# Interleaving the weight slabs so that TensorE loads weights with a step of two, four or eight elements

## The chip, the cores and the metric

The kernel runs on one core of one Trainium2 chip. The metric is the device time of one execution in microseconds (us); lower is better. All matrix work is done on TensorE (PE in the profile, with its weight loads on a row of their own, PEld). VectorE (DVE) and ScalarE (ACT) prepare operands and finish results, SyncE (SP) issues the transfers from device memory.

## What is computed

One layer of a sequence model for 256 time steps of 2048 channels, all in float32. Cut to what matters:

```python
z = rmsnorm(x, g1) @ w_in + b_in              # 2048 -> 7 * 2048
xa, ya, cb, cc, cx, ga, gb = split(z)
xa = rg_lru(causal_conv4(xa))                 # gates: 8 blocks of 256x256
out_a = (xa * gelu(ya)) @ w_pa                # 2048 -> 2048
out_b = (cb * causal_conv3(cc * cx)) @ w_pb   # 2048 -> 2048
x = x + (sigmoid(ga) * out_a + sigmoid(gb) * out_b) @ w_o
u = square(relu(rmsnorm(x, g2) @ w_mlp1))     # 2048 -> 8192
x = x + u @ w_mlp2                            # 8192 -> 2048
return rmsnorm(x, gf)
```

## The kernel before

**Layout.** Channels lie on the 128 partitions and the 256 time steps along the free dimension, so an activation of 2048 channels is 16 tiles of 128 x 256. A weight matrix is cut, on the host, into slabs: a slab holds 8 blocks of 128 x 128 (8 row blocks of one column block), that is 128 partitions x 1024 float32 numbers or 512 KB. In a slab of before, block k takes the columns from k x 128 to k x 128 + 127, one block after the other.

**Two parts for precision.** Every float32 number is split into a high part, rounded to the format that TensorE takes at full speed, and a low part, the remainder. For weights the class `Weights` does this: SP transfers a slab into a `raw` tile (one of 4), ACT casts it into `whi` (L52), DVE subtracts to give `wlo` (L53). There are four buffers of each, and slabs are made three ahead of their use. Activations are held as tiles `a` of 128 x 2 x 256 with the high part in `a[:, 0]` and the low part in `a[:, 1]`.

**The inner loop.** `product` makes one tile of 128 output channels. For each block it runs two matmuls: the *hi* matmul, with the block of `whi` as stationary operand and both parts of the activation as 512 moving columns (L260), and the *lo* matmul, with the block of `wlo` and the high part of the activation, 256 moving columns (L261). Each of the two has a weight load of its own, of 128 x 128 numbers. The result lies in one PSUM bank of 2 x 256 numbers; the lo matmul adds to one of its halves, and `added` (L266, L268) sums the halves. A *pair* below is one hi and one lo matmul.

**Stages**, in this order, with the tiles of 128 outputs and the pairs of each: the first four tiles of w_in, written out in `first_four` (L289, L290) while the slabs are still arriving; the rest of w_in for the branches, with small gate matmuls for the recurrence (L370 to L372) after each group; a merge stage that for each of 16 tiles takes two tiles of w_in, one of w_pb and one of w_pa; w_o; and then w_1 and w_2, each in two halves `h` (32 tiles of w_1, 16 tiles of w_2, twice). A tile from 2048 channels has 16 pairs; a tile of w_2 in one half has 32. The very last tile of w_2 is made in pieces by `rows` (L460, L461), its last 18 blocks for one half of the time steps and then for the other, so that the final norm and the stores of the first half overlap.

**Two irregular places.** In the first half of w_2 every second tile is made `turned`: apart from its first and last block the lo matmul is issued ahead of the hi matmul (L257, L258). And in w_1 the lo matmul adds to half 1 of the bank for h = 0 and to half 0 for h = 1 (`side`).

**The end.** After the last stores are issued, 20 further matmuls run whose result nobody reads (L532, L534). They take blocks of `whi` as stationary operand, and four at a time differ in the weight columns (128 or 32) and in the moving operand (activation, weights, one element broadcast to 512 columns, and bfloat16 ones).

Instructions on each engine run in the order in which the engine was given them; DVE and ACT get their slab splits with a priority that moves them ahead in that order.

Of the kernel before, what the change touches and what calls it, by code (L numbers as in the profile page):

```python
# [9 lines left out]
F32 = mybir.dt.float32  # L10
# [4 lines left out]
P = 128  # L15
S = 256
D = 2048
NT = D // P
# [3 lines left out]
HALF = 8  # L22
# [2 lines left out]
AHEAD = 300  # L25
WAKE = 9
SPLIT = 18

PARAMS = [("g1", NT), ("g2", NT), ("gf", NT), ("b_in", 7 * NT), ("ca_w", 4 * NT), ("ca_b", NT),
          ("br", NT), ("bi", NT), ("lam", NT), ("cb_w", 3 * NT), ("eye", P)]  # L30
# [50 lines left out]
def trunk(ctx: ExitStack, tc: tile.TileContext, xT, xt, par, w_in, w_lru, w_pa, w_pb, w_o, w_1, w_2, out):  # L81
    nc = tc.nc
# [5 lines left out]
    wk = ctx.enter_context(tc.tile_pool(name="wk", bufs=3))  # L88
    psz = ctx.enter_context(tc.tile_pool(name="psz", bufs=6, space=bass.MemoryType.PSUM))
    psl = ctx.enter_context(tc.tile_pool(name="psl", bufs=2, space=bass.MemoryType.PSUM))  # L90
# [6 lines left out]
    def moving(i):  # L97
        return big.tile([P, NT, 2, S], F32R, name="big%d" % i)
# [32 lines left out]
    def pc(name, j):  # L131
        return pr[:, OFF[name] + j:OFF[name] + j + 1]

    def split(dst, src):

        nc.scalar.copy(dst[:, 0, :], src)
        nc.vector.tensor_tensor(dst[:, 1, :], src, dst[:, 0, :].bitcast(F32), ALU.subtract)  # L137

    def scaled_split(dst, src, g):
        nc.scalar.activation(dst[:, 0, :], src, AF.Copy, scale=g)  # L140
        nc.vector.scalar_tensor_tensor(dst[:, 1, :], src, g, dst[:, 0, :].bitcast(F32), ALU.mult, ALU.subtract)
# [12 lines left out]
    def total(parts):  # L154

        ps = psl.tile([P, 512], F32, name="psl")
        for i, sq in enumerate(parts):
            nc.tensor.matmul(ps[:, :S], ones, sq, start=i == 0, stop=i == len(parts) - 1)
        return ps[:, :S]
# [13 lines left out]
    xg = moving(0)  # L173
# [17 lines left out]
    for i in range(NT // 2):  # L191
        load_x(2 * i, 2)
        c, o = divmod(i, HALF // 2)
# [13 lines left out]
    for i, n in enumerate(("xc", "gy", "cb", "cc", "gate0", "gate1", "q", "v")):  # L207
        h, q = divmod(i, 4)
# [5 lines left out]
    def squares(src, j):  # L214

        if j == 0:
            nc.scalar.activation(ssq, src, AF.Square)
        else:
            sq = wk.tile([P, S], F32, name="s")
            nc.scalar.activation(sq, src, AF.Square)  # L220
            nc.vector.tensor_tensor(ssq, ssq, sq, ALU.add)
# [21 lines left out]
        nc.vector.scalar_tensor_tensor(s2, sd, 2.0, s2, ALU.mult, ALU.add)  # L243
        nc.vector.tensor_scalar(s4, s2, -4.0, None, ALU.mult)

    def product(acts, k0, nh, side=1, turned=False):

        ps = psz.tile([P, 2, S], F32, name="psz")
        n = nh * HALF
        for c in range(nh):  # L250
            hi, lo = W.take()
            for k in range(HALF):
                a = acts(k0 + c * HALF + k)
                i = c * HALF + k
                b = slice(k * P, (k + 1) * P)
                if turned and 0 < i < n - 1:
                    nc.tensor.matmul(ps[:, side, :], lo[:, b], a[:, 0, :], start=False, stop=False)  # L257
                    nc.tensor.matmul(ps, hi[:, b], a, start=False, stop=False)  # L258
                else:
                    nc.tensor.matmul(ps, hi[:, b], a, start=i == 0, stop=False)  # L260
                    nc.tensor.matmul(ps[:, side, :], lo[:, b], a[:, 0, :], start=False, stop=i == n - 1)  # L261
        return ps

    def added(ps):
        low = wk.tile([P, S], F32, name="low")
        nc.scalar.copy(low, ps[:, 1, :])  # L266
        t = wk.tile([P, S], F32, name="t")
        nc.vector.tensor_tensor(t, ps[:, 0, :], low, ALU.add)  # L268
        return t
# [4 lines left out]
        nc.scalar.activation(dst, t, func, bias=pc("b_in", j))  # L274

    def z_product():
        return product(lambda k: xg[:, k], 0, 2)

    def z_tile(j, dst, func):
        z_done(z_product(), j, dst, func)  # L280

    def first_four():

        four = [psz.tile([P, 2, S], F32, name="psz") for _ in range(4)]
        for k in range(NT):
            c = slice(k % 2 * P, (k % 2 + 1) * P)
            for m in range(4):
                hi, lo = fhi[:, k // 2, m, c], flo[:, k // 2, m, c]
                nc.tensor.matmul(four[m], hi, xg[:, k], start=k == 0, stop=False)  # L289
                nc.tensor.matmul(four[m][:, 1, :], lo, xg[:, k, 0, :], start=False, stop=k == NT - 1)  # L290
        return four

    early = first_four()

    def first_norm():
# [16 lines left out]
    ua = moving(1)  # L312
    ub = moving(2)
    with places:
# [5 lines left out]
        for g in range(NB):  # L320
# [3 lines left out]
            for m in range(2):  # L324
                j = 2 * g + m
# [5 lines left out]
                c = xc[:, m, :]  # L331
# [17 lines left out]
            for m in range(2):  # L349
                j = 2 * g + m  # L350
# [3 lines left out]
                c = cc[:, m, :]  # L354
# [8 lines left out]
            hi, lo = W.take()  # L363
            gates = []
            for q in range(2):
                ps = psl.tile([P, 2, S], F32, name="psl")
# [6 lines left out]
                t = w1.tile([P, 2, S], F32, name="gate%d" % q)  # L373
# [3 lines left out]
            r, i = gates  # L377
# [21 lines left out]
    mg = big2.tile([P, NT, 2, S], F32R, name="mg")  # L399
    for j in range(NT):  # L400
        sa = wk.tile([P, S], F32, name="s")
        sb = wk.tile([P, S], F32, name="s")
        z_tile(Z_GA + j, sa, AF.Sigmoid)
        z_tile(Z_GB + j, sb, AF.Sigmoid)
        tb = added(product(lambda k: ub[:, k], 0, 2))
        nc.vector.tensor_tensor(sb, sb, tb, ALU.mult)
        ta = added(product(lambda k: ua[:, k], 0, 2))
        nc.vector.tensor_tensor(sa, sa, ta, ALU.mult)
        nc.vector.tensor_tensor(sa, sa, sb, ALU.add)
        split(mg[:, j], sa)  # L410

    xh = moving(0)
    for j in range(NT):
        t = added(product(lambda k: mg[:, k], 0, 2))
        nc.vector.tensor_tensor(x[:, j, :], x[:, j, :], t, ALU.add)
        scaled_split(xh[:, j], x[:, j, :], pc("g2", j))
        squares(x[:, j, :], j)

    for h in range(2):
        u = [big2.tile([P, NT, 2, S], F32R, name="mg") if h == 1 and c == 0 else moving(c + 1) for c in range(2)]  # L420
        for f in range(NF // 2):
            t = added(product(lambda k: xh[:, k], 0, 2, side=1 - h))
            v = wk.tile([P, S], F32, name="s")
            nc.vector.scalar_tensor_tensor(v, t, 0.0, t, ALU.max, ALU.mult)  # L424
            if h == 1:
                nc.vector.tensor_tensor(v, v, rs, ALU.mult)
            split(u[f // NT][:, f % NT], v)
            if h == 0 and f == 0:
                nc.vector.tensor_scalar(rs, total([ssq]), 1.0 / D, EPS, ALU.mult, ALU.add)
                nc.vector.reciprocal(rs, rs)  # L430
        for j in range(NT - h):
            t = added(product(lambda k: u[k // NT][:, k % NT], 0, 4, turned=h == 0 and j % 2 == 1))
            if h == 0:
                nc.vector.tensor_tensor(t, t, rs, ALU.mult)
            nc.vector.tensor_tensor(x[:, j, :], x[:, j, :], t, ALU.add)
            if h == 1:
                squares(x[:, j, :], j)
                if j == NT - 2:
                    nc.scalar.activation(sink, ssq[:, 0:1], AF.Sqrt)
                nc.scalar.activation(x[:, j, :], x[:, j, :], AF.Copy, scale=pc("gf", j))  # L440

    bf4 = wk.tile([P, 512], mybir.dt.bfloat16, name="s")
    bf = bf4[:, :P]
    nc.gpsimd.memset(bf4, 1.0)

    w = [W.take() for _ in range(4)]
    nk = 4 * HALF

    def rows(k0, k1, c, between=()):

        ps = psz.tile([P, 2, S], F32, name="psz")
        for k in range(k0, k1):
            if k in between:
                between[k]()
            hi, lo = w[k // HALF]
            a = u[k // NT][:, k % NT, :, c]
            b = slice(k % HALF * P, (k % HALF + 1) * P)
            nc.tensor.matmul(ps[:, :, c], hi[:, b], a, start=k == k0, stop=False)  # L460
            nc.tensor.matmul(ps[:, 1, c], lo[:, b], a[:, 0, :], start=False, stop=k == k1 - 1)  # L461
        return ps
# [43 lines left out]

    k0 = nk - SPLIT
    got = []
    t = added(rows(0, k0, slice(0, S)))
# [13 lines left out]
    store(1, by, 2, (5, 5, 4), (nc.sync, nc.scalar))  # L523


    hi = w[3][0]
    still = psl.tile([P, 512], F32, name="psl")
    for cols, moved in ((128, u[1][:, 3]), (32, u[1][:, 3]), (128, hi[:, 0:512].rearrange("p (a b) -> p a b", a=2)),
                        (128, u[1][:, 3, 0:1, 0:1].broadcast_to([P, 2, S])), (0, None)):
        for i in range(4):  # L530
            if cols:
                nc.tensor.matmul(still[:cols, :], hi[:, i * P:i * P + cols], moved, start=True, stop=True)  # L532
            else:
                nc.tensor.matmul(still, bf, bf[:, 0:1].broadcast_to([P, 512]) if i > 1 else bf4, start=True, stop=True)  # L534


def _slabs(w):


    k, n = w.shape  # L540
    w = w.reshape(k // (HALF * P), HALF, P, n // P, P)
    return np.ascontiguousarray(w.transpose(3, 0, 2, 1, 4)).reshape(n // P, k // (HALF * P), P, HALF * P)


def _cols(v):
# [33 lines left out]
```

## Time and profile before

| | |
|---|---|
| time, median of 2 runs | 1657.09 us (1656.47 to 1657.7) |
| profiled execution | 1657.53 us, of which its span, first to last instruction, is 1655.4 us |
| PE / PEld busy | 1648.0 us (100%) / 1448.9 us (88%) |
| DVE / ACT busy | 1123.7 us (68%) / 867.1 us (52%) |
| mean granted TensorE clock | 0.998 |
| read from device memory | 310.62 MB, 189 GB/s over the span |

Busy time is the union of an engine's instruction times. Matmuls overlap each other in the trace, since one begins while the one ahead is still draining, so the mean duration of a matmul (392 ns for hi) is longer than the distance from its start to the next start. The distances are what adds up to the span.

### The profile page before, as it was taken

Reading aid. Unit: us, or ns where it says so; the run is one execution under the profiler, and the core shown is the slowest. Engines: PE = TensorE matmul, PEld = TensorE weight load, DVE = VectorE, ACT = ScalarE, POOL = GpSimd, SP = SyncE. Lnnn points to the kernel's source line nnn. Section 1 sums busy time; section 2 is a strip of 40 time slices with the busy share of each in tenths; the row PEclk is TensorE's granted clock in tenths of the full one; section 3 lists DMA queues with packets and bytes.
Section 4 is the critical chain, followed back from the end, with each engine's and each line's share of the span. In section 5 each row is a group of like instructions: output and inputs, shape, how many; then the busy total and the mean of one; then the engine's idle time right before and its main releaser. Section 6 shows DMA issues by size and latency. Waiting matters only on the chain.

```text
span 1655.4 us, 24421 instructions
## 1 busy us (share of the span) xinstructions
PE 1648.0 (100%) x9500; PEld 1448.9 (88%) x9500; DVE 1123.7 (68%) x1628; ACT 867.1 (52%) x1272; POOL 3.9 (0%) x38
## 2 busy tenths in 40 slices
PE   9999999999999999999999999999999999999998
PEld 8888888888888888888888888888888888888887
DVE  5979878978976666566667766665555677765554
ACT  7756666666765444444455444443334444444442
POOL 0000000000000000000000000000000000000000
PEclk9999999999999999999999999999999999999999
DMA  9665555556556555555555555555555555665553
GB/s 310 195 200 190 186 190 189 187 178 204 190 180 192 190 191 187 187 189 189 191 184 191 185 191 190 187 189 188 189 191 190 189 186 189 190 190 191 190 187 95
DMA packets 94228, 314.31 MB, mean 190 GB/s; under 512 B 10016, under 2 KB 18336, under 8 KB 94112
## 3 DMA queue, kind: packets, MB, share of 16 engines
q1 hardware_dynamic: 93184, 312.29, 58.2%
q8 instruction: 74, 1.21, 0.3%
q10 hardware_dynamic: 928, 0.46, 0.1%
q14 instruction: 42, 0.34, 0.1%
HBM read 310.62 MB, written 2.10 MB: 189 GB/s over the span
## 4 chain that ended last, share of the span: by engine, by line
PE 99%; DVE 1%; DMA 0%; issue 0%; SPq 0%; DVEq 0%; ACT 0%
PE psz L260 59%; PE psz L261 30%; PE psz L258 3%; PE psz L257 2%; PE psz L289 1%; PE psz L460 1%; PE psz L290 0%; PE psl L371 0%; PE psl L372 0%; PE psl L370 0%; PE psl L532 0%; DMA raw<-w_in_s 0%; PE psz L461 0%; DVE wlo L53 0%; DVE x L502 0%; DVE v L392 0%
## 5 line engine op out<-in xcount | busy, mean ns | idle before, releaser
L260 PE MATMUL psz<-big,whi 128*128 128x512 f32 x3776 | 1318.7, 392 | 0.2 <-DVE big L137 0.2
L261 PE MATMUL psz<-big,wlo 128*128 128x256 f32 x3776 | 1059.1, 280 | 0.0
L53 DVE TENSOR_TENSOR wlo<-raw,whi 128x1024 fp32r<-128x1024 f32 x576 | 703.2, 1223 | 488.1 <-ACT whi L52 487.4
L52 ACT CAST whi<-raw 128x1024 fp32r<-128x1024 f32 x576 | 604.1, 1049 | 751.2 <-issue 418.1
L260 PEld LDWEIGHTS psz<-big,whi 128*128 128x128 f32 x3776 | 708.9, 188 | 159.7 <-DVE big L137 0.5
L261 PEld LDWEIGHTS psz<-big,wlo 128*128 128x128 f32 x3776 | 709.9, 188 | 0.4
L260 PE MATMUL psz<-mg,whi 128*128 128x512 f32 x496 | 173.5, 393 | 0.0
L261 PE MATMUL psz<-mg,wlo 128*128 128x256 f32 x496 | 138.8, 280 | 0.0
L260 PEld LDWEIGHTS psz<-mg,whi 128*128 128x128 f32 x496 | 93.1, 188 | 21.0 <-DVE mg L137 0.2
L268 DVE TENSOR_TENSOR t<-psz,low 128x256 f32<-128x256 f32 x256 | 105.9, 417 | 2.8 <-ACT low L266 2.8
L261 PEld LDWEIGHTS psz<-mg,wlo 128*128 128x128 f32 x496 | 93.5, 189 | 0.1
L266 ACT COPY low<-psz 128x256 f32<-128x256 f32 x256 | 93.3, 366 | 0.0
L258 PE MATMUL psz<-big,whi 128*128 128x512 f32 x240 | 84.4, 394 | 0.0
L257 PE MATMUL psz<-big,wlo 128*128 128x256 f32 x240 | 67.2, 280 | 0.0
L258 PEld LDWEIGHTS psz<-big,whi 128*128 128x128 f32 x240 | 45.1, 188 | 10.2
L273 DVE TENSOR_TENSOR t<-t,rs 128x256 f32<-128x256 f32 x112 | 47.1, 422 | 2.2
L257 PEld LDWEIGHTS psz<-big,wlo 128*128 128x128 f32 x240 | 45.2, 188 | 0.3
L424 DVE SCALAR_TENSOR_TENSOR s<-t 128x256 f32<-128x256 f32 x64 | 27.2, 425 | 2.1
L382 DVE RECIPROCAL q<-q 128x512 f32<-128x512 f32 x8 | 26.8, 3344 | 0.0
L289 PE MATMUL psz<-big,big 128*128 128x512 f32 x64 | 23.0, 416 | 1.8 <-ACT big L52 1.8
L334 DVE SCALAR_TENSOR_TENSOR xc<-xa,pr,xc 128x256 f32<-128x256 f32 x48 | 22.3, 477 | 0.0
L137 DVE TENSOR_TENSOR big<-s,big 128x256 fp32r<-128x256 f32 x48 | 20.1, 418 | 0.0
(148 smaller groups left out, 662.1 us busy)
## 6 DMA issues: line engine op xcount, KB each, us to landing
raw<-w_s SPq DMA_DIRECT2D x256, 512.0 KB, 4.2
raw<-w_in_s SPq DMA_DIRECT2D x216, 512.0 KB, 3.5
raw<-w_pb_s SPq DMA_DIRECT2D x32, 512.0 KB, 3.6
raw<-w_pa_s SPq DMA_DIRECT2D x32, 512.0 KB, 3.5
raw<-w_o_s SPq DMA_DIRECT2D x32, 512.0 KB, 3.5
raw<-w_in_s SPq DMA_DIRECT2D x16, 256.0 KB, 5.8
raw<-w_lru_s SPq DMA_DIRECT2D x8, 512.0 KB, 3.6
x<-xT SPq DMA_DIRECT2D x8, 256.0 KB, 5.8
```

What stands on the lines that cost most here:

```text
L52: self.nc.scalar.copy(hi, raw)
L53: self.nc.vector.tensor_tensor(lo, raw, hi.bitcast(F32), ALU.subtract)
L257: nc.tensor.matmul(ps[:, side, :], lo[:, b], a[:, 0, :], start=False, stop=False)
L258: nc.tensor.matmul(ps, hi[:, b], a, start=False, stop=False)
L260: nc.tensor.matmul(ps, hi[:, b], a, start=i == 0, stop=False)
L261: nc.tensor.matmul(ps[:, side, :], lo[:, b], a[:, 0, :], start=False, stop=i == n - 1)
L266: nc.scalar.copy(low, ps[:, 1, :])
L268: nc.vector.tensor_tensor(t, ps[:, 0, :], low, ALU.add)
L273: nc.vector.tensor_tensor(t, t, rs, ALU.mult)
L289: nc.tensor.matmul(four[m], hi, xg[:, k], start=k == 0, stop=False)
L382: nc.vector.reciprocal(q, q)
L424: nc.vector.scalar_tensor_tensor(v, t, 0.0, t, ALU.max, ALU.mult)
```

## The change

Each matrix gets a step: 2 for w_in and w_2, 4 for w_pb and w_1, 8 for w_pa and w_o. On the host, the slab's blocks are interleaved in groups of `step`: column 0 of the group's first block, column 0 of the second and so on, then column 1 of each. A block's 128 columns then lie `step` elements apart, and every weight load reads them so. Size, number and order of the slabs, their transfers and their splits stay as they are, and the recurrence's gate weights stay contiguous. `turned` and `side` are gone: the hi matmul always comes first and the lo matmul always adds to half 1. The 20 matmuls at the end and the tile of ones for them are removed.

```diff
+STEP = {"w_in": 2, "w_pa": 8, "w_pb": 4, "w_o": 8, "w_1": 4, "w_2": 2}
...
-    def product(acts, k0, nh, side=1, turned=False):
+    def columns(k, step):
+
+        b = k // step * step * P + k % step
+        return slice(b, b + (P - 1) * step + 1, step)
+
+    def product(acts, k0, nh, step):
...
-                b = slice(k * P, (k + 1) * P)
-                if turned and 0 < i < n - 1:
-                    nc.tensor.matmul(ps[:, side, :], lo[:, b], a[:, 0, :], start=False, stop=False)
-                    nc.tensor.matmul(ps, hi[:, b], a, start=False, stop=False)
-                else:
-                    nc.tensor.matmul(ps, hi[:, b], a, start=i == 0, stop=False)
-                    nc.tensor.matmul(ps[:, side, :], lo[:, b], a[:, 0, :], start=False, stop=i == n - 1)
+                b = columns(k, step)
+                nc.tensor.matmul(ps, hi[:, b], a, start=i == 0, stop=False)
+                nc.tensor.matmul(ps[:, 1, :], lo[:, b], a[:, 0, :], start=False, stop=i == n - 1)
...
-            c = slice(k % 2 * P, (k % 2 + 1) * P)
+            c = columns(k % 2, STEP["w_in"])
...
-            t = added(product(lambda k: xh[:, k], 0, 2, side=1 - h))
+            t = added(product(lambda k: xh[:, k], 0, 2, STEP["w_1"]))
...
-            t = added(product(lambda k: u[k // NT][:, k % NT], 0, 4, turned=h == 0 and j % 2 == 1))
+            t = added(product(lambda k: u[k // NT][:, k % NT], 0, 4, STEP["w_2"]))
...
-            b = slice(k % HALF * P, (k % HALF + 1) * P)
+            b = columns(k % HALF, STEP["w_2"])
...
-    hi = w[3][0]
-    still = psl.tile([P, 512], F32, name="psl")
-    for cols, moved in ((128, u[1][:, 3]), (32, u[1][:, 3]), (128, hi[:, 0:512].rearrange("p (a b) -> p a b", a=2)),
-                        (128, u[1][:, 3, 0:1, 0:1].broadcast_to([P, 2, S])), (0, None)):
...
-def _slabs(w):
+def _slabs(w, step):
...
-    w = w.reshape(k // (HALF * P), HALF, P, n // P, P)
-    return np.ascontiguousarray(w.transpose(3, 0, 2, 1, 4)).reshape(n // P, k // (HALF * P), P, HALF * P)
+    w = w.reshape(k // (HALF * P), HALF // step, step, P, n // P, P)
+    return np.ascontiguousarray(w.transpose(4, 0, 3, 1, 5, 2)).reshape(n // P, k // (HALF * P), P, HALF * P)
```

The order of instructions on DVE, ACT and SP is the same before and after, line numbers aside; POOL loses one fill of a tile with ones. PE's order changes at two places. The first is each second tile of w_2 in the half h = 0. There PE had (output, activation, weights, size; the numbers belong to buffers):

```order
L260 MATMUL psz<-big_9275,whi_11001 128x512
L261 MATMUL psz<-big_9275,wlo_11002 128x256
L257 MATMUL psz<-big_9275,wlo_11002 128x256
L258 MATMUL psz<-big_9275,whi_11001 128x512
L257 MATMUL psz<-big_9275,wlo_11002 128x256
```

and now has, at the same place, with the two lines of `product` renumbered:

```order
L262 MATMUL psz<-big_9275,whi_11001 128x512
L263 MATMUL psz<-big_9275,wlo_11002 128x256
L262 MATMUL psz<-big_9275,whi_11001 128x512
L263 MATMUL psz<-big_9275,wlo_11002 128x256
L262 MATMUL psz<-big_9275,whi_11001 128x512
```

The second block's lo matmul has moved behind its hi matmul, and so on through the tile, so that hi and lo alternate everywhere. The second place is the end of the program. Before, behind the last lo matmul of the last tile, the last sum of squares and the spread of its result:

```order
L461 MATMUL psz<-big_12498,wlo_15700 128x128
L484 MATMUL psl<-ones,s 128x1
L496 MATMUL psl<-pr,cm_15845 128x128
L532 MATMUL psl<-big_12498,whi_15699 128x512 x4
L532 MATMUL psl<-big_12498,whi_15699 32x512 x4
L532 MATMUL psl<-whi_15699 128x512 x4
L534 MATMUL psl<-s 128x512
L574 UNCONDITIONAL_BRANCH
```

and now:

```order
L459 MATMUL psz<-big_12498,wlo_15698 128x128
L482 MATMUL psl<-ones,s 128x1
L494 MATMUL psl<-pr,cm_15843 128x128
L561 UNCONDITIONAL_BRANCH
```

PE now reaches the end of its program right after the spread. The rows do not show the step of a weight load; it stands only in the slices of the diff.

More of the change, by code (lines that the diff above doesn't have):

```diff
@@ L276, in z_product @@
     def z_product():
-        return product(lambda k: xg[:, k], 0, 2)
+        return product(lambda k: xg[:, k], 0, 2, STEP["w_in"])
     def z_tile(j, dst, func):
@@ L404, in trunk @@
         z_tile(Z_GB + j, sb, AF.Sigmoid)
-        tb = added(product(lambda k: ub[:, k], 0, 2))
+        tb = added(product(lambda k: ub[:, k], 0, 2, STEP["w_pb"]))
         nc.vector.tensor_tensor(sb, sb, tb, ALU.mult)
-        ta = added(product(lambda k: ua[:, k], 0, 2))
+        ta = added(product(lambda k: ua[:, k], 0, 2, STEP["w_pa"]))
         nc.vector.tensor_tensor(sa, sa, ta, ALU.mult)
@@ L413, in trunk @@
     for j in range(NT):
-        t = added(product(lambda k: mg[:, k], 0, 2))
+        t = added(product(lambda k: mg[:, k], 0, 2, STEP["w_o"]))
         nc.vector.tensor_tensor(x[:, j, :], x[:, j, :], t, ALU.add)
@@ L440, in trunk @@
                 nc.scalar.activation(x[:, j, :], x[:, j, :], AF.Copy, scale=pc("gf", j))
-    bf4 = wk.tile([P, 512], mybir.dt.bfloat16, name="s")
-    bf = bf4[:, :P]
-    nc.gpsimd.memset(bf4, 1.0)
     w = [W.take() for _ in range(4)]
@@ L523, in trunk @@
     store(1, by, 2, (5, 5, 4), (nc.sync, nc.scalar))
-    hi = w[3][0]
-    still = psl.tile([P, 512], F32, name="psl")
-    for cols, moved in ((128, u[1][:, 3]), (32, u[1][:, 3]), (128, hi[:, 0:512].rearrange("p (a b) -> p a b", a=2)),
-                        (128, u[1][:, 3, 0:1, 0:1].broadcast_to([P, 2, S])), (0, None)):
[L530 to L534, printed above, removed]
-def _slabs(w):
+def _slabs(w, step):
     k, n = w.shape
-    w = w.reshape(k // (HALF * P), HALF, P, n // P, P)
-    return np.ascontiguousarray(w.transpose(3, 0, 2, 1, 4)).reshape(n // P, k // (HALF * P), P, HALF * P)
+    w = w.reshape(k // (HALF * P), HALF // step, step, P, n // P, P)
+    return np.ascontiguousarray(w.transpose(4, 0, 3, 1, 5, 2)).reshape(n // P, k // (HALF * P), P, HALF * P)
 def _cols(v):
@@ L562 @@
             norm1_g, norm2_g, final_g, b_in, conv_a_w, conv_a_b, lru_br, lru_bi, lru_lam, conv_b_w, np.eye(P, dtype=np.float32))], 1)),
-        "w_in_s": _slabs(np.asarray(w_in)[0]),
+        "w_in_s": _slabs(np.asarray(w_in)[0], STEP["w_in"]),
         "w_lru_s": np.ascontiguousarray(lru).reshape(NB, P, HALF * P),
-        "w_pa_s": _slabs(np.asarray(w_pa)[0]),
-        "w_pb_s": _slabs(np.asarray(w_pb)[0]),
-        "w_o_s": _slabs(np.asarray(w_o)[0]),
-        "w_1_s": _slabs(np.asarray(w_mlp1)[0]),
-        "w_2_s": _slabs(np.asarray(w_mlp2)[0]),
+        "w_pa_s": _slabs(np.asarray(w_pa)[0], STEP["w_pa"]),
+        "w_pb_s": _slabs(np.asarray(w_pb)[0], STEP["w_pb"]),
+        "w_o_s": _slabs(np.asarray(w_o)[0], STEP["w_o"]),
+        "w_1_s": _slabs(np.asarray(w_mlp1)[0], STEP["w_1"]),
+        "w_2_s": _slabs(np.asarray(w_mlp2)[0], STEP["w_2"]),
     }
```

## Prediction

> **What bounds the kernel now.** I read the page's busy times and its chain of waits first, then the groups by line, then what PE waited for, and last the times at which matmuls and weight loads start.
>
> ```profile
> span 1655.4 us, 24421 instructions
> ...
> PE 1648.0 (100%) x9500; PEld 1448.9 (88%) x9500; DVE 1123.7 (68%) x1628; ACT 867.1 (52%) x1272; POOL 3.9 (0%) x38
> ...
> PEclk9999999999999999999999999999999999999999
> ...
> PE 99%; DVE 1%; DMA 0%; issue 0%; SPq 0%; DVEq 0%; ACT 0%
> ...
> L260 PE MATMUL psz<-big,whi 128*128 128x512 f32 x3776 | 1318.7, 392 | 0.2 <-DVE big L137 0.2
> L261 PE MATMUL psz<-big,wlo 128*128 128x256 f32 x3776 | 1059.1, 280 | 0.0
> L53 DVE TENSOR_TENSOR wlo<-raw,whi 128x1024 fp32r<-128x1024 f32 x576 | 703.2, 1223 | 488.1 <-ACT whi L52 487.4
> ```
>
> PE is 99% of the chain that ended last, at full clock, and its two main lines wait for others for 0.2 us in all. So the time is the number of pairs times the distance from pair to pair, and anything that lengthens or shortens that distance enters the time undiluted. DVE, the next busiest engine, has a third of the span free. The stages run at one pace (windows of equal length: busy us of PE, PEld, DVE, ACT and POOL with their instruction counts, clock, share of the DMA engines, GB/s; w_1, w_2 for h = 0, then w_1 for h = 1):
>
> ```profile
> 940.00:1100.00 160.00, 160.00 (x921) 140.75 (x920) 101.91 (x145) 76.99 (x115) 0.00 (x0) 1.00 0.59 188
> 1120.00:1280.00 160.00, 160.00 (x920) 140.20 (x919) 87.34 (x100) 63.63 (x71) 0.00 (x0) 1.00 0.58 189
> 1300.00:1460.00 160.00, 160.00 (x920) 140.75 (x919) 113.69 (x173) 77.17 (x115) 0.00 (x0) 1.00 0.60 188
> ```
>
> 920 matmuls are 460 pairs: 160/460 = 0.348 us a pair. Within a pair (the timeline of PE, then of PEld: start, duration):
>
> ```profile
> 802.10 0.39 PE L260 MATMUL psz<-big,whi 128*128 128x512 f32 x1
> 802.33 0.28 PE L261 MATMUL psz<-big,wlo 128*128 128x256 f32 x1
> 802.45 0.39 PE L260 MATMUL psz<-big,whi 128*128 128x512 f32 x1
> ...
> 802.10 0.19 PEld L261 LDWEIGHTS psz<-big,wlo 128*128 128x128 f32 x1
> 802.33 0.19 PEld L260 LDWEIGHTS psz<-big,whi 128*128 128x128 f32 x1
> 802.45 0.19 PEld L261 LDWEIGHTS psz<-big,wlo 128*128 128x128 f32 x1
> ```
>
> The hi matmul occupies 0.230 us (802.10 to 802.33), the lo matmul 0.118 (what is left of 0.348). A load starts when a matmul starts and fetches the weights of the next one: lo weights come in under a hi matmul, hi weights under a lo matmul. How fast can loads follow each other? The last tile tells, where the moving operands are half as long and hide less:
>
> ```profile
> 1641.47 0.19 PEld L460 LDWEIGHTS psz<-big,whi 128*128 128x128 f32 x1
> ...
> 1642.05 0.19 PEld L461 LDWEIGHTS psz<-big,wlo 128*128 128x128 f32 x1
> ```
>
> Those are six loads in a row, five distances in 0.58 us: **0.116 us a load**. So a load under a lo matmul has 0.118 us of cover and needs 0.116; under a hi matmul it needs 0.116 of 0.230. The lo side has no slack, and that is where a slower load would show at once.
>
> **The change part by part.**
>
> *The counts.* From the loops: w_in 112 tiles x 16 = 1792 pairs and w_2 1024 at step 2, together 2816; w_1 64 x 16 = 1024 and w_pb 256 at step 4, together 1280; w_pa and w_o 256 each at step 8, together 512. In all 4608 pairs, of which 1792 have a step of 4 or 8.
>
> *Step 2.* No strided load is in the trace, so its cost is an estimate between bounds. The moving operand is read at 512 contiguous numbers in 0.230 us, 0.45 ns each. A load takes 0.116/128 = 0.91 ns per number. At step 2 it advances two positions per number, 0.45 ns per position: just the pace at which PE is seen to read the same memory. I take **0**.
>
> *Steps 4 and 8.* At 0.116 us a load would have to advance 0.23 ns or 0.11 ns per position, two and four times the pace that any row shows. If the shown pace is the memory's limit for fresh places, each number of a load then costs what two cost now. The nearest rows for a slower load are the ones at half clock near the end (windows with clock 0.50, then loads of 128 and of 32 columns in them):
>
> ```profile
> 1647.80:1649.30 1.50, 1.50 (x4) 1.19 (x5) 1.50 (x3) 0.00 (x0) 0.00 (x0) 0.50 1.00 282
> 1649.50:1650.80 1.30, 1.30 (x4) 0.51 (x3) 0.10 (x1) 0.00 (x0) 0.00 (x0) 0.50 1.00 279
> ...
> L532 PEld LDWEIGHTS psl<-big,whi 128*128 128x128 f32 x4 | 1.2, 320 | 1.7 <-issue 1.5
> ...
> L532 PEld LDWEIGHTS psl<-big,whi 128*32 128x32 f32 x3 | 0.5, 170 | 0.8 <-issue 0.8
> ```
>
> 96 more columns cost 150 ns, 1.56 ns a column, at full clock half of it: 0.100 us of the 0.116 grow with the columns. Doubled per column the load takes 0.216 us; if all of it doubles, 0.232. I take the middle, 0.224. Under a lo matmul 0.224 + 0.002 us replaces 0.118: **+0.108 us**; under a hi matmul 0.224 still fits into 0.230: 0. That is 1792 x 0.108 = **+193.5 us**, from 1792 x 0.100 = 179 to, where 0.232 also overruns the hi matmul, 1792 x 0.118 = 211. The lower end is not 0 but a gain (below); the upper end is a load that walks through every position at 0.45 ns: 0.230 at step 4, 0.46 at step 8, there on both sides of the pair: 1280 x 0.112 + 512 x 0.572 = +436 us. I choose the doubling because the memory's pace does matter to PE in this trace:
>
> ```profile
> 1652.37 0.40 PE L532 MATMUL psl<-whi 128*128 128x512 f32 x1
> 1652.61 1.03 PE L532 MATMUL psl<-big,whi 128*128 128x512 f32 x4
> ...
> L532 PE MATMUL psl<-big,whi 128*128 128x512 f32 x4 | 1.0, 380 | 0.0
> ```
>
> The first moves 512 different numbers and holds PE for 0.24 us; the four behind it repeat one number 512 times and follow at (1.03 - 0.38)/3 = 0.217 us, 0.38 being the mean duration of one. Fetching one place again is cheaper than going on to fresh ones.
>
> [...]
>
> *`turned` and `side`.* Nothing: the window from 1120 to 1280, where half the tiles are turned, and the two windows of w_1, one with each side, have the same 920 matmuls in 160 us. *DVE, ACT, SP.* They read and write slabs contiguously as before (L53 1223 ns), in the same order; if PE slows they have more room.
>
> *The 20 matmuls at the end.* SP's wait for them and for the last store:
>
> ```profile
> SPq L574 <- DMA outT<-x: 3.2, 1, 3.2
> ...
> SPq L574 <- PE psl L534: 1.1, 1, 1.1
> ```
>
> SP, which ends the program, waited for the stores and then 1.1 us more for PE: **-1.1 us**; what is late then is the last store.
>
> *Sum*, against the profiled execution's own 1657.53 us (2.1 outside its span, 0.44 above the median): 1657.5 + 193.5 - 1.1 = 1849.9, so **1850 us**, by its own bounds 1835 to 1868.
>
> **The rivals.**
>
> *Any step is free* (0.33): the load takes its numbers one by one at 0.91 ns, slower than the memory answers even from fresh places. Then only the end changes: 1656 us. For it: a load needs half the pace of the moving operand, and 0.45 ns may be TensorE's own limit and not the memory's. The same holds if the step never reaches the instruction in a form that matters.
>
> *Faster* (0.10): the 0.217 against 0.230 us says that some 13 ns of each hi matmul come from its moving reads. If they come from meeting the load's reads in the same memory, a stepped load, at step 2 in stride with the moving operand, could avoid the meetings. With 13 ns saved everywhere: 1656 - 4608 x 0.013 = 1596 us; on step 2 alone 1656 - 37 = 1619. It decides for "faster" from 33 us, 7 ns a pair. Against it: the repeated number changes the moving reads themselves too, so nothing shows that a load is what they meet, and more places per load can as well mean more meetings. [...]
>
> *A price per distance* (0.10): loads whose stationary operand is one number broadcast to 128 columns follow at (0.61 - 0.274)/3 = 0.112 us:
>
> ```profile
> 37.98 0.61 PE L309 MATMUL psl<-pr,m 128*128 128x128 f32 x4
> ...
> L309 PE MATMUL psl<-pr,m 128*128 128x128 f32 x4 | 0.6, 274 | 0.0
> ```
>
> That is 0.004 less than 0.116. If these 4 ns are the price of passing 128 positions, steps 2, 4 and 8 add 4, 12 and 28 ns a load: 2816 x 0.004 + 1280 x 0.012 + 512 x 0.028 = 41, so 1697 us.
>
> *Worse than forecast* (0.05): the walk through every position, 1656 + 436 = 2092 us.
>
> **How the numbers follow.** The forecast has 0.42. It and the free step are close because neither is seen in the trace; I put the forecast ahead since the lo side has no slack and any price lands there. A measurement of this kernel tells about 2% from no change. Faster by over 2%: 0.10; within 2%: 0.33; slower: 0.42 + 0.10 + 0.05 = 0.57. Range: from 1640 (the free step with a little gained) to 1870 (the forecast's upper bound); outside lie faster and worse, 0.15. As signs differ, the forecast's own range is 1835 to 1868.
>
> **What would show it.** Distances between starts by stage: 0.348 us a pair in w_in and w_2, 0.456 in w_1, w_pb, w_pa and w_o, the growth all behind lo matmuls; a longer duration of PEld in these stages than 0.19; w_pa like w_pb. The forecast is wrong if w_1 keeps 0.348, if step 2 grows too, or if step 8 costs more than step 4.

## Result and profile after

The changed kernel takes 1889.27 us (median of 2 runs, 1888.86 to 1889.68) against 1657.09: a ratio of 1.140, with an interval of 1.135 to 1.145. It is slower by 232 us. The profiled execution took 1888.86 us with a span of 1886.9, so 231.5 us more span. Its page:

```profile
span 1886.9 us, 24379 instructions
...
PE 1874.4 (99%) x9480; PEld 1768.3 (94%) x9480; DVE 1124.5 (60%) x1628; ACT 866.1 (46%) x1272; POOL 3.4 (0%) x37
...
PE 99%; DVE 0%; DMA 0%; SPq 0%; ACT 0%; DVEq 0%; issue 0%
...
L262 PE MATMUL psz<-big,whi 128*128 128x512 f32 x4016 | 1599.3, 441 | 0.0
L263 PE MATMUL psz<-big,wlo 128*128 128x256 f32 x4016 | 1134.1, 282 | 0.0
```

PE still is 99% of the chain, at the same clock (0.997 after 0.998), and DVE and ACT are busy for as long as before, 1124 and 866 us: all the new time is inside PE. Its own busy time grew by 226 us and that of its loads, PEld, by 319. Windows of single stages show where (w_o at step 8; w_1 at step 4; w_2 at step 2):

```profile
920.00:1020.00 100.00, 100.00 (x413) 100.00 (x412) 50.94 (x77) 39.43 (x65) 0.00 (x0) 1.00 0.39 134
1050.00:1250.00 200.00, 200.00 (x856) 200.00 (x855) 94.80 (x135) 70.90 (x106) 0.00 (x0) 1.00 0.42 140
1280.00:1440.00 160.00, 160.00 (x912) 143.16 (x911) 86.12 (x100) 63.59 (x71) 0.00 (x0) 1.00 0.58 186
```

A pair, two matmuls, takes 2 x 100/413 = 0.484 us at step 8, 0.467 at step 4 and 0.351 at step 2, against 0.348 before. (A window also counts the matmuls that reach over its edges, so a pair comes out up to 3 ns short in one of 100 us or less: the hi matmuls of w_o start 0.487 us apart on average over the whole stage, and that is the figure used further down.) In the two slow stages PEld, the second busy time of a row, is busy without a break. The timeline of w_1 (PE, then PEld):

```profile
1150.13 0.52 PE L262 MATMUL psz<-big,whi 128*128 128x512 f32 x1
1150.49 0.28 PE L263 MATMUL psz<-big,wlo 128*128 128x256 f32 x1
1150.61 0.51 PE L262 MATMUL psz<-big,whi 128*128 128x512 f32 x1
...
1150.02 0.31 PEld L262 LDWEIGHTS psz<-big,whi 128*128 128x128 f32 x1
1150.23 0.33 PEld L263 LDWEIGHTS psz<-big,wlo 128*128 128x128 f32 x1
1150.49 0.31 PEld L262 LDWEIGHTS psz<-big,whi 128*128 128x128 f32 x1
1150.70 0.33 PEld L263 LDWEIGHTS psz<-big,wlo 128*128 128x128 f32 x1
```

A load lasts 0.31 to 0.33 us where it lasted 0.19, and four loads start within 0.68 us. The records put all the growth behind the hi matmul: 0.36 us from its start to the lo matmul (1150.13 to 1150.49), while 0.12 from lo to hi is as before. Taken at its word that says that the matmul with 512 moving columns has become slower, with a lo load running beside it. Two theories follow. **A**: a load got longer, and it is exposed where it outlasts the matmul it runs under; the hi matmul's recorded start is not the moment its weights are in (at 1150.13 the load that began at 1150.02 is not done). **B**: a stepped load slows the moving reads beside it.

### The profile page after: what moved, and what is told of

The parts are those of the page before. It is cut to its first block, busy times and chain, and to the rows that moved or that the text cites. A ratio compares the mean times of both kernels' runs of the same rounds, so it can differ in the third digit from the quotient of the medians.

```text
span 1886.9 us, 24379 instructions
## 1 busy us (share of the span) xinstructions
PE 1874.4 (99%) x9480; PEld 1768.3 (94%) x9480; DVE 1124.5 (60%) x1628; ACT 866.1 (46%) x1272; POOL 3.4 (0%) x37
## 4 chain that ended last, share of the span: by engine, by line
PE 99%; DVE 0%; DMA 0%; SPq 0%; ACT 0%; DVEq 0%; issue 0%
PE psz L262 67%; PE psz L263 29%; PE psz L291 1%; PE psz L458 1%; PE psz L292 0%; PE psl L373 0%; PE psl L374 0%; PE psl L372 0%; DMA raw<-w_in_s 0%; PE psz L459 0%; DVE x L500 0%; PE psl L494 0%; ACT big L53 0%; DVEq L561 0%; PE psl L311 0%
## 5 line engine op out<-in xcount | busy, mean ns | idle before, releaser
L262 PE MATMUL psz<-big,whi 128*128 128x512 f32 x4016 | 1599.3, 441 | 0.0
L262 PEld LDWEIGHTS psz<-big,whi 128*128 128x128 f32 x4016 | 963.4, 240 | 92.9
L263 PEld LDWEIGHTS psz<-big,wlo 128*128 128x128 f32 x4016 | 997.4, 248 | 0.0
L262 PE MATMUL psz<-mg,whi 128*128 128x512 f32 x496 | 209.4, 461 | 0.0
L262 PEld LDWEIGHTS psz<-mg,whi 128*128 128x128 f32 x496 | 130.0, 262 | 8.6
L263 PEld LDWEIGHTS psz<-mg,wlo 128*128 128x128 f32 x496 | 134.6, 271 | 0.0
L137 ACT CAST big<-s 128x256 fp32r<-128x256 f32 x48 | 19.3, 402 | 0.0
L373 PE MATMUL psl<-xs,whi 128*128 128x256 f32 x64 | 18.1, 282 | 0.0
L374 PE MATMUL psl<-xs,wlo 128*128 128x256 f32 x64 | 18.0, 281 | 0.0
L372 PE MATMUL psl<-xs,whi 128*128 128x256 f32 x64 | 17.9, 280 | 0.0
```

The costliest lines, as they stand in the source:

```text
L263: nc.tensor.matmul(ps[:, 1, :], lo[:, b], a[:, 0, :], start=False, stop=i == n - 1)
```

## Experiments

Pair times below are worked out as above, twice the window's length over its count of matmuls. From the second experiment on each time is that of a single run.

**Steps alone.** All steps 1, the rest of the change kept:

```diff
-STEP = {"w_in": 2, "w_pa": 8, "w_pb": 4, "w_o": 8, "w_1": 4, "w_2": 2}
+STEP = {"w_in": 1, "w_pa": 1, "w_pb": 1, "w_o": 1, "w_1": 1, "w_2": 1}
```

> The changed kernel with every step set to 1: contiguous slabs again, without turned and side and without the 20 matmuls at the end. If the steps alone made the slow-down: 0.348 us a pair in all stages and 1656 us, ratio 0.999 to before. If turned, side or the end took part: over 1665.

1655.41 us, ratio 0.9994 with an interval of 0.9984 to 1.0003, and 0.348 us a pair, here in w_1 for h = 1:

```profile
1290.00:1450.00 160.00, 160.00 (x920) 140.82 (x920) 114.77 (x174) 76.25 (x114) 0.00 (x0) 1.00 0.56 189
```

`turned`, `side` and the 20 matmuls at the end are worth nothing that can be measured: the step makes all of the slow-down.

**One step everywhere.** The same line with 4, then with 8, for all but w_in, which keeps 2.

> Step 4 for all matrices but w_in (2, since the first four tiles are loaded in pairs of blocks). Theory A, loads follow one another and each load at step 4 takes 0.234: 0.352 us a pair in w_in, 0.468 in every other stage, w_2 and w_pa included: 1656 + 1792 x 0.004 + 2816 x 0.120 = 2001 us. If what w_1 showed belongs to that stage and not to the step: w_2 stays near 0.352.

> Step 8 for all matrices but w_in (2). If step 8 itself is dearer than step 4 (0.487 against 0.468 in the changed kernel): 1656 + 7 + 2816 x 0.138 = 2052 us, and 0.487 in w_1 too. Rival: the difference came from the activation tiles of w_pa and w_o: then w_1 and w_2 show 0.468 at step 8 too, about 2010 us.

2005.8 and 2060.63 us. Step 4, in w_1 and w_2 (first two rows), then step 8 in w_1 and w_2:

```profile
1040.00:1240.00 200.00, 200.00 (x856) 200.00 (x856) 95.52 (x136) 70.94 (x106) 0.00 (x0) 1.00 0.40 140
1280.00:1480.00 200.00, 200.00 (x856) 200.00 (x856) 82.01 (x96) 59.07 (x66) 0.00 (x0) 1.00 0.40 140
```

```profile
1050.00:1250.00 200.00, 200.00 (x821) 200.00 (x822) 91.13 (x130) 69.26 (x104) 0.00 (x0) 1.00 0.39 136
1310.00:1510.00 200.00, 200.00 (x821) 200.00 (x821) 77.93 (x90) 56.97 (x64) 0.00 (x0) 1.00 0.38 135
```

w_2, at 0.351 in the changed kernel, now has the 0.467 of w_1, and w_1 takes 0.487 at step 8. The price goes with the step and not with the matrix, and step 8 costs more than step 4. Both runs end 5 to 9 us later than expected; that is the last tile, and the section on the hardware comes back to it.

**Which load.** From the kernel of step 4, one of the two loads of a pair made contiguous again (`d` is the slice of before; the weights that it reads are not the block's):

```diff
+                d = slice(k * P, (k + 1) * P)
-                nc.tensor.matmul(ps[:, 1, :], lo[:, b], a[:, 0, :], start=False, stop=i == n - 1)
+                nc.tensor.matmul(ps[:, 1, :], lo[:, d], a[:, 0, :], start=False, stop=i == n - 1)
```

and the other way round, `hi[:, d]` with `lo[:, b]`. Both edits are in `product`: the last tile, which `rows` makes, keeps step 4 for both of its loads, and w_in keeps step 2 for the load that stays stepped.

> The kernel of step 4 with the low parts' loads reading 128 neighbouring columns of the interleaved slab (not the reference's weights), so that only hi loads, which run under lo matmuls, are stepped. Theory A (a load is exposed where it outlasts the matmul it runs under): 0.230 + 0.234 = 0.464 us a pair outside w_in: 1656 + 7 + 2816 x 0.116 = 1990 us. Theory B (a stepped load slows the moving reads beside it; after the change the distance behind hi grew, that behind lo did not): the hi matmul is beside contiguous loads now and keeps 0.230, so about 1663 to 1720.

> The kernel of step 4 with the high parts' loads reading 128 neighbouring columns (not the reference's weights), so that only lo loads, which run under hi matmuls, are stepped. Theory A: 0.234 against 0.230 of cover: 0.352 us a pair: 1656 + 2816 x 0.004 = 1667 us. Theory B: the hi matmul goes to 0.349: 1656 + 2816 x 0.119 = 1991 us.

1992.86 and 1686.34 us. In w_1, hi alone stepped:

```profile
1030.00:1230.00 200.00, 200.00 (x861) 181.38 (x862) 95.30 (x136) 72.24 (x109) 0.00 (x0) 1.00 0.41 142
```

and lo alone stepped:

```profile
940.00:1100.00 160.00, 160.00 (x905) 160.00 (x904) 101.74 (x142) 75.16 (x114) 0.00 (x0) 1.00 0.54 186
```

0.465 and 0.354 us a pair. Nearly the whole price of step 4 hangs on the hi loads, whose cover is the short lo matmul; the lo load, the one beside the hi matmul, costs 0.006. B is refuted by both runs. A's pairs hold within 2 ns: 0.465 for 0.464 and 0.354 for 0.352, which puts the stepped load at 0.235 (0.465 - 0.230) and 0.236 (0.354 - 0.118). The second run's time still missed A's 1667 by 19 us, more than its predicted growth: the 2 ns of 2784 pairs are 6 us, the step of 2 in w_in, which the sum left out, about 5 (0.003 on 1728 pairs), and the last tile takes 24.6 us from its first hi matmul to its last (1647.7 to 1672.3), 11 more than at step 1.

**More cover.** The lo matmul moves both halves of the activation, which adds the product of the two low parts:

```diff
-                nc.tensor.matmul(ps[:, 1, :], lo[:, b], a[:, 0, :], start=False, stop=i == n - 1)
+                nc.tensor.matmul(ps, lo[:, b], a, start=False, stop=i == n - 1)
```

> All steps 1, and the lo matmul in product moves both parts of the activation, 512 columns instead of 256 (it adds the product of the low parts, which the kernel otherwise leaves out). Both theories: two matmuls of 0.230: 0.460 us a pair, 1656 + 4512 x 0.112 = 2161 us. If part of the 0.230 is waiting for the hi load under the short lo matmul: less, down to 2 x 0.217 = 0.434 and 2044 us.

> Steps 2 (w_in) and 4 (all others), with the lo matmul of 512 columns. Theory A: where step 4 rules, the pair is two loads, 2 x 0.234 = 0.468, and the 256 added columns cost nothing; only w_in grows, by 1728 x 0.108: about 2001 + 187 = 2188 us. Theory B: the added columns take their time everywhere: 0.58 a pair outside w_in and about 2500 us.

2173.91 and 2208.97 us, 13 and 21 us above A's sums: the pair is 0.463 where 0.460 was counted, 0.471 where 0.468 was, and the second has the long last tile too. In w_1 at step 1, then at step 4:

```profile
1230.00:1430.00 200.00, 200.00 (x864) 162.48 (x863) 98.03 (x135) 74.87 (x108) 0.00 (x0) 1.00 0.41 142
```

```profile
1230.00:1430.00 200.00, 200.00 (x849) 200.00 (x849) 97.91 (x136) 73.58 (x106) 0.00 (x0) 1.00 0.40 140
```

At step 1 the added 256 columns cost 0.463 - 0.348 = 0.115 us a pair; at step 4 they cost 0.471 - 0.467 = 0.004. There the pair is two loads long, 2 x 0.234 or 0.2355 us, with either lo matmul. The first run also says that 0.230 for a hi matmul hides no waiting for weights: two matmuls of 512 columns, each with a load half as long as its cover, take 0.2315 each on average.

**The price of each step.** The slabs stay contiguous, and the loads of each stage read with a step of their own, starting at column k:

```diff
+        if step == 0:
+            return w[:, k:k + 1].broadcast_to([P, P])
+        b = k % 8 if step > 1 else k * P
+        return w[:, b:b + (P - 1) * step + 1:step]
```

> The slabs stay contiguous, and the loads read with a step of 3 in w_in, 5 in w_pb, 6 in w_pa, 7 in w_o, 0 (one column for all 128) in w_1 for h = 0 and 1 for h = 1, 6 in w_2 for h = 0 and 5 for h = 1, so the weights used are not the reference's. Theory of blocks of four numbers: a load costs 1.83 ns (0.234/128) for every block it enters, never less than 0.115: step 3 enters 96 blocks, 0.176, a pair 0.230 + 0.176 = 0.406; steps 5, 6, 7 enter 128, 0.468 to 0.487. Theory of a threshold at four: step 3 like step 2, 0.352. Theory of the prediction, 0.45 ns a position: 0.405 at step 3 as well, but 0.58, 0.69 and 0.80 at 5, 6 and 7. Step 0: 0.344 to 0.348.

In order, steps 3 (a part of w_in without gate matmuls), 7, 0, 6 and 5:

```profile
150.00:200.00 50.00, 50.00 (x245) 50.00 (x245) 35.32 (x54) 25.38 (x37) 0.14 (x2) 1.00 0.44 158
1010.00:1110.00 100.00, 100.00 (x426) 100.00 (x425) 51.79 (x80) 40.58 (x66) 0.00 (x0) 1.00 0.39 139
1130.00:1290.00 160.00, 160.00 (x925) 140.84 (x924) 103.29 (x145) 77.40 (x116) 0.00 (x0) 1.00 0.55 191
1320.00:1520.00 200.00, 200.00 (x865) 200.00 (x865) 81.60 (x93) 60.12 (x67) 0.00 (x0) 1.00 0.40 142
1730.00:1930.00 200.00, 200.00 (x868) 200.00 (x868) 81.34 (x96) 72.35 (x97) 0.00 (x0) 1.00 0.39 141
```

| step | 0 | 1 | 2 | 3 | 4 | 5 | 6 | 7 | 8 |
|---|---|---|---|---|---|---|---|---|---|
| us a pair | 0.346 | 0.348 | 0.351 | 0.408 | 0.467 | 0.461 | 0.462 | 0.469 | 0.487 |

The staircase fits the theory of blocks of four numbers, in which a load pays for every block that it enters. At step 4, where every number lies in another block, a load is half of 2 x 200/856 us, 1.83 ns for each of its 128 numbers. Step 3 enters 96 blocks: 96 x 1.83 = 0.176, and with the hi matmul's 0.230 that makes 0.406, an estimate from step 4; measured 0.408 (0.411 by the starts of the matmuls, this window being short). Step 2 enters 64: 64 x 1.83 = 0.117, an estimate that puts it just where the price of blocks passes the 0.116 of a contiguous load. From 4 on each number would have its own block, and the curve is flat within 0.006 up to 6, with a rise at 7 and 8; step 0 lies 0.002 below step 1 (925 matmuls in 160 us against 920). The blocks themselves are not shown: a price per position that stops growing at step 4 gives the same estimates, half of 0.234 at step 2 and three quarters at step 3. Nor is it shown whether numbers or bytes count, since every run loads float32. A price per position that goes on growing is ruled out: it would have a load at step 8 take twice that at step 4, 0.468, and it takes 0.2435.

**Without moving reads.** Both matmuls of a pair move one number, broadcast to all columns (so nothing here is the reference's product), at steps 1, 2, 4 and 8:

```diff
+                one = a[:, 0:1, 0:1].broadcast_to([P, 2, S])
-                nc.tensor.matmul(ps, hi[:, b], a, start=i == 0, stop=False)
-                nc.tensor.matmul(ps[:, 1, :], lo[:, b], a[:, 0, :], start=False, stop=i == n - 1)
+                nc.tensor.matmul(ps, hi[:, b], one, start=i == 0, stop=False)
+                nc.tensor.matmul(ps[:, 1, :], lo[:, b], one[:, 0, :], start=False, stop=i == n - 1)
```

> All steps 1, and in product both matmuls move one number of the activation, broadcast to all 512 or 256 columns (so the products are not the reference's); the loads are as before. If the 17 ns that a hi matmul takes beyond the fastest seen come from reading 512 different numbers: 0.217 behind hi and 0.112 to 0.116 behind lo (the load's own pace), 0.331 a pair: 1655 - 4512 x 0.017 = 1578 us. If they belong to the matmul or to the change of weights: 0.348 and 1655 us.

> The same moving of one number, with step 2 everywhere. If the 4 ns of step 2 are the load's own (0.120 against 0.115, just over what the lo matmul covers): 4 ns above the run at step 1, 1578 + 18 = 1596 us. If they come from meeting the moving reads: no difference to step 1.

> The same moving of one number, steps 2 (w_in) and 4. If a load at step 4 takes 0.234 by itself: the pair stays two loads, 0.468, w_in 0.335: 1655 + 2784 x 0.120 - 1728 x 0.013 = 1967 us. If part of the 0.234 is waiting for the moving reads, so that the load alone doubles the 0.100 to 0.107 us that grow with the columns: 2 x 0.213 = 0.427 and about 1852 us.

> The same moving of one number, steps 2 (w_in) and 8. If the 10 ns a load by which step 8 is dearer than step 4 are its own: 2 x 0.244 = 0.487 and about 2022 us. If they come from meeting the moving reads: the same time as step 4 with one number moved.

1573.99, 1601.28, 1974.75 and 1999.31 us. The windows of w_2, one from each run in this order:

```profile
1060.00:1210.00 150.00, 150.00 (x911) 137.72 (x910) 85.97 (x100) 63.46 (x72) 0.00 (x0) 1.00 0.59 199
```

```profile
1080.00:1230.00 150.00, 150.00 (x894) 141.10 (x893) 84.52 (x98) 62.07 (x70) 0.00 (x0) 1.00 0.58 195
```

```profile
1250.00:1450.00 200.00, 200.00 (x858) 200.00 (x859) 82.75 (x96) 59.18 (x67) 0.00 (x0) 1.00 0.40 140
```

```profile
1260.00:1460.00 200.00, 200.00 (x843) 200.00 (x843) 80.25 (x93) 59.14 (x67) 0.00 (x0) 1.00 0.40 139
```

0.329, 0.336, 0.466 and 0.474 us a pair. Step 2 costs 0.007 without real moving reads, so its few nanoseconds are the load's own: 0.336 less the 0.217 of a hi matmul that repeats one number leaves 0.119. A load at step 4 takes 0.233 with them or without. Step 8 without them is 0.237 a load, with them 0.2435: of the 10 ns by which it is dearer than step 4, about 6 are there only beside real moving reads and 4 are its own. Why 8 is dearer than 5 or 6 at all was not settled.

## Why the prediction was right and wrong

The time, 1889 us, lies above the predicted 1850 and outside the range, which ended at 1870. Direction and mechanism held: the loads at steps 4 and 8 outlast the lo matmul, and step 2 is all but free. The sizes did not. Term by term:

| term | predicted us | measured us |
|---|---|---|
| step 4, 1280 pairs | 138 | 1280 x (0.467 - 0.348) = 152 |
| step 8, 512 pairs | 55 | 512 x (0.487 - 0.348) = 71 |
| step 2, 2816 pairs | 0 | 2816 x (0.351 - 0.348) = 8 |
| end, `turned`, `side` | -1.1 | 1653.7 - 1655.4 = -1.7 (spans of step 1 and before; within the scatter of runs) |
| sum | 192 | 230; the spans differ by 231.5 |

*The counts, the stage bound and the missing slack on the lo side* were right; the pair of runs with one stepped load shows that side as the place.

*The failed step is the size of a load at steps 4 and 8*, put at 0.224 us and at most 0.232. It was built from the price of a column at half clock: of the 0.116 us of a load, the 0.100 that seemed to grow with the columns was doubled, and the middle taken between that and doubling all of it. The runs show another size: 0.234 at step 4, 1.83 ns for every number, a size that it keeps at half clock (45 matmuls in 10 us there and at full clock, further down), and 0.2435 at step 8. Both lie above the upper bound, so the range came out too narrow. That a doubling came so near is in part luck: the reason given for it, a pace of 0.45 ns a position, gives 0.230 at step 4 but 0.46 at step 8 by itself, and the runs at steps 5 to 8 rule it out.

*With it falls "under a hi matmul 0.224 still fits into 0.230: 0".* At 0.234 and 0.2435 the lo load too outlasts its cover, by 4 and 13.5 ns; that, over 1792 pairs, is 1280 x 0.004 + 512 x 0.0135 = 12 us. The rest of the two terms is the hi load's longer exposure.

*Step 2 at 0* was 0.003 us a pair short, small but on 2816 pairs.

*"The growth all behind lo matmuls"* was wrong as a reading of the trace, though right as a cause. *"w_pa like w_pb"* was wrong: step 8 is dearer, one of the signs that the prediction had named against itself.

*The rivals.* "Any step is free" is refuted by all runs with steps from 3, at 0.408 us a pair and more. "Faster" named a real quantity, since a hi matmul takes 0.231 us with its own moving reads and 0.216 with one repeated number, but a step does not win it back: 0.351 us a pair at step 2 against 0.348. "A price per distance" gets the wrong shape, and so does the walk through every position, "worse than forecast", with its 0.46 us a load at step 8. That steps 4 and 8 pay alike, as the prediction had it, is off by 0.020 us a pair (0.467 and 0.487). Whether a load takes time from the matmul it runs under, as "faster" supposed, is not decided here, since no run shows a matmul slowed by a load. The other direction is seen: beside real moving reads a load takes 0.234 us at step 4 against 0.233, and 0.2435 at step 8 against 0.237.

## What to carry to other kernels

Lay weights out so that the 128 columns of a stationary operand are neighbours; with float32 a step of 2 cost about 1% of a pair here (0.351 against 0.348 us), and from 4 on a load took twice as long (0.234 against 0.116 us at step 4). Whether that is seen depended on the matmul the load ran under, 0.354 us a pair under the hi matmul and 0.465 under the lo matmul: compare the distance of loads where they limit (a tile with short moving operands shows it, here the last one with 0.116 us) with the matmul of each kind, and sum over the pair. A growth that the trace shows behind one matmul can belong to the load of that same matmul, under the one before, as the 0.36 us behind the hi matmul did here: step one of the two loads to find out.

## What the runs showed of the hardware

**A load at step 4 does not follow TensorE's clock.** In the run at step 4 the last tile, too, is bound by loads. Ten microseconds of it on either side of the moment the granted clock (the third number from the right) fell to half:

```profile
1967.00:1977.00 10.00, 10.00 (x45) 10.00 (x44) 3.26 (x6) 4.11 (x7) 0.00 (x0) 1.00 0.00 1
1980.00:1990.00 10.00, 10.00 (x45) 10.00 (x44) 1.29 (x7) 0.97 (x3) 0.00 (x0) 0.50 0.00 0
```

45 matmuls each: the loads keep their pace at half the clock, while the contiguous loads of the prediction's rows lasted 320 ns there and 188 at full clock (L260 on the page of before). That speaks against any estimate that scales a stepped load with the clock. The rows also show the clock falling while PE is recorded busy throughout, with short matmuls behind long loads; in the changed kernel, at step 2, the last tile ran 72 matmuls in 10 us at full clock (the row below). What made it fall was not tested.

```profile
1861.00:1871.00 10.00, 10.00 (x72) 9.46 (x71) 3.46 (x7) 3.99 (x7) 0.00 (x0) 1.00 0.01 2
```

The last tile is also where the runs with one step everywhere missed their sums by 5 to 9 us. From its first hi matmul to its last it took 13.7 us at step 1 (1628.4 to 1642.1), 24.5 at step 4 (1967.2 to 1991.7) and 25.3 at step 8 (2021.3 to 2046.6): 11 to 12 us more, where the sums had 32 pairs of 0.120 or 0.138, 4 us. Most of its matmuls are half as long and cover less of their loads, so a pair of them grows from 0.23 to 0.47 us at step 4, two loads in both cases.

**Moving reads cost time even with every load covered.** Moving one number instead of 512 shortens the pair from 0.348 to 0.329 us, 5% of the kernel (1655.41 to 1573.99 us), while two covered matmuls of 512 different numbers took 0.2315 us each, against the 0.217 of one repeated number in the prediction's rows. By the starts in w_2, a hi matmul takes 0.216 us with one number and 0.231 at step 1, a lo matmul 0.114 and 0.1175, there close to the pace of the loads, 0.116. Whether reading different numbers is slower by itself or by meeting the load's reads was not separated. No layout tried here gets at that time.
